# Branch B's k in 512 columns, two merge-gate chunks ahead of branch B's q, and a shorter attention step

## The chip, the core and the metric

The kernel runs on one core of a Trainium2 chip. A core has a matrix engine (TensorE, "PE" in the profile, with a queue of its own for loading weights, "PEld"), a vector engine (VectorE, "DVE"), a scalar engine (ScalarE, "ACT"), GpSimd ("POOL"), and SyncE ("SP"), which here issues every transfer between HBM and the on-chip memory. The engines run at the same time and wait for one another by semaphores. The metric is the device time of one execution in microseconds (us): 963.23 before, the median of three runs (961.96 to 965.53).

## What is computed

One layer of a block with two attention branches, for 1024 positions of width 1024, all in fp32. Cut to what matters:

```python
h = rms_norm(x, norm_w) * (1 + scale) + shift             # scale, shift, gate from c
(cq, ckv, k_rope, gate_a, q_b, k_b, v_b, f_b, gate_b, mg_a, mg_b) = split(h @ w_in)
# branch A: latent attention, 8 heads, chunk-causal
q = rms_norm(cq) @ w_uq ; kv = rms_norm(ckv) @ w_ukv      # then norms per head, rotary parts
y_a = mla_attention(q, kv, k_rope) * silu(gate_a)
# branch B: attention with a forget gate, 8 heads of 64
qb, kb = rms_norm(q_b), rms_norm(k_b)                     # per head
y_b = fox_attention(qb, kb, v_b, log_sigmoid(f_b)) * silu(gate_b)
merged = sigmoid(mg_a) * (y_a @ w_branch_a) + sigmoid(mg_b) * (y_b @ w_branch_b)
x = x + gate * (merged @ w_out)
```

The change touches how `q_b`, `k_b` and `v_b` (512 columns each) and the first of the columns of `gate_a`, `gate_b`, `mg_a`, `mg_b` (24 chunks of 128) are projected, and when.

## The kernel before

**Tiling.** A matrix product is done in three passes: each operand is split into a high and a low part, and high x high, high x low and low x high are summed in one PSUM bank. `split` (L105) makes the parts: ScalarE writes the high part (L115), VectorE subtracts for the low part (L116). The inner dimension of 1024 takes 8 steps, so one output tile costs 24 matmuls. `hT_hi` and `hT_lo` hold the normalized input transposed. Weights are loaded by `load_w` (L102 issues it) into slots of 128x1024 fp32, 0.524 MB.

**Branch B's projection** is the generator `g1b` (L805). q and k are four column chunks of 256 (`ci` 0 and 1 are q, 2 and 3 are k). Each has 8 sequence tiles, two in one bank, so 192 matmuls of 128x256; tile names are `b`. Then come ScalarE's copy (L844) and square (L845) of a 128x512 tile, VectorE's reduction (L849) and, once per chunk, the root (`rsqrt`, L84) and the scaling (L858). The scaled tiles go to DRAM as `qb_d` and `kb_d`. v is one chunk of 512: 8 tiles of 24 matmuls of 128x512, named `bv`, stored as `vb_d`. `store_b` (L891) issues a store only at the next call, and SP issues strictly in the order of the program.

**Order.** It is written out by hand. Attention and the projections of branch A are written as steps. Between them `fill_to(t)` draws matmuls from the generator `fillers` (L924) until a model clock, `pe_time`, which adds up a time for each matmul, reaches `t`. `fillers` yields first all of `g1b`, then 24 chunks `("t", c)` of the gates and merge gates (48 matmuls of 128x512 each, tile `f`), then the chunks of the branch outputs. The order of `g1b` against the steps thus follows from counts of model time.

**Attention** has 16 heads (8 of A, then 8 of B), each of 12 steps. `prep_a` and `prep_b` load a pair of heads' q and k as [positions, columns] (`qs_u`, `ks_u`, 0.524 MB), transpose them on PE (`qt`, `kt`) and, for branch A, load the rotary rows (`q_u` and `k_u` from `qr_d` and `kr_d`, 0.131 MB each). `scores` makes `s`, its maximum, the exponential (ScalarE) and the scaling (GpSimd); `turn` transposes the probabilities (`pt`) and splits them (`pp_u`); the product with v (`v_u`) is `o`. Each step moves the due time on by `STEP` = 2490 model ns, and fill comes up to `due - 600` and `due`. At attention's start, ahead of the fifth score, the rest of `g1b` is drawn whatever the model time (L1281: `while not self.g1b_done: next(self.fill)`). After the last step the rest of the fill runs without a pause.

Of the kernel before, what the change touches and what calls it, by code (L numbers as in the profile page):

```python
# [22 lines left out]
KT = 8  # L23
ST = 8
# [48 lines left out]


class Net:
    STEP = 2490.0

    def __init__(self, ctx, tc, t):
        self.ctx, self.tc, self.nc, self.t = ctx, tc, tc.nc, t
# [725 lines left out]
    def g1b(self, hook):  # L805

        nc, t, U, Hs = self.nc, self.t, self.U, self.Hs
        w = {}

        def load(ci):  # L810
# [5 lines left out]
        load(0)  # L816
        yield False
        w[0] = [self.split(x, f"b0_{e}") for e, x in enumerate(w[0])]
        yield False
        for ci in range(4):  # L820
            kind, half = ci // 2, ci % 2
            for sp in range(4):
                if sp == 0:
                    load(ci + 1)
                if sp in (1, 2) or (ci, sp) == (3, 3):
                    w[ci + 1][sp - 1] = self.split(w[ci + 1][sp - 1], f"b{ci + 1}_{sp - 1}")
                acc = self.fbank(f"b{ci}_{sp}")
                for i in range(2):
                    st = 2 * sp + i
                    sl = slice(st * P, (st + 1) * P)  # L830
                    for kt in range(KT):
                        wh, wl = w[ci][kt // 4]
                        for e, (a, b) in enumerate(((self.hT_hi, wh), (self.hT_hi, wl), (self.hT_lo, wh))):
                            self.mm(acc[:, i * 256:(i + 1) * 256], a[:, kt, sl], b[:, kt % 4],
                                    kt == 0 and e == 0, kt == KT - 1 and e == 2)
                            if (ci, sp, i, kt, e) == (3, 3, 1, 3, 2):
                                U.put(*w[3][0])
                                w[4][3] = self.split(w[4][3], "b4_3")
                            if e == 2 and kt % 2 and (i, kt) != (1, KT - 1):
                                yield False  # L840
                a3 = acc.rearrange("p (g d) -> p g d", d=64)
                o = Hs.get([P, 8, 64], F32, f"bo{ci}_{sp}")
                sq = Hs.get([P, 8, 64], F32, f"bsq{ci}_{sp}")
                nc.scalar.copy(o, a3)  # L844
                nc.scalar.activation(sq, o, AF.Square)  # L845
                if sp == 0:
                    ssq = self.sp.tile([P, 32], F32, tag="bssq", bufs=2, name=f"bssq{ci}")
                    outs = []
                nc.vector.reduce_sum(ssq[:, 8 * sp:8 * sp + 8], sq, axis=AX.X)  # L849
                Hs.put(sq)  # L850
                self.store_b()
                outs.append(o)
                if sp == 3:
                    r = self.rsqrt(ssq, 32, 64, f"b{ci}_{sp}")
                    dst = (self.qb_d, self.kb_d)[kind]
                    items = []
                    for j, o in enumerate(outs):
                        nc.vector.tensor_tensor(out=o, in0=o, op=ALU.mult,  # L858
                                                in1=r[:, 8 * j:8 * j + 8].unsqueeze(2).broadcast_to([P, 8, 64]))
                        items.append((dst[2 * j:2 * j + 2, :, half * 256:half * 256 + 256].rearrange("s p c -> p s c"),  # L860
                                      o.rearrange("p (s h) d -> p s (h d)", s=2), (Hs, o)))
                    self.store_b(*items)
                if sp == 3:
                    for pair in w.pop(ci)[ci // 3:]:
                        U.put(*pair)
                yield 1000.0
        w = w[4]
        for st in range(ST):
            if st in (1, 5):
                hook()  # L870
            acc = self.fbank(f"bv_{st}")
            sl = slice(st * P, (st + 1) * P)
            for kt in range(KT):
                wh, wl = w[kt // 2]
                for e, (a, b) in enumerate(((self.hT_hi, wh), (self.hT_hi, wl), (self.hT_lo, wh))):
                    self.mm(acc, a[:, kt, sl], b[:, kt % 2], kt == 0 and e == 0, kt == KT - 1 and e == 2)
                if st == ST - 1 and kt % 2:
                    U.put(*w[kt // 2])
                if kt < KT - 1:
                    yield False  # L880
            a3 = acc.rearrange("p (g d) -> p g d", d=64)
            vhl = U.get([P, 8, P], F32R, f"bvhl_{st}")
            nc.scalar.copy(vhl[:, :, 0:64], a3)
            nc.vector.tensor_tensor(out=vhl[:, :, 64:128], in0=a3, in1=vhl[:, :, 0:64].bitcast(F32), op=ALU.subtract)
            self.store_b((self.vb_d[st], vhl.bitcast(F32), (U, vhl)))
            if st == ST - 1:
                self.store_b()
                self.g1b_done = True
            yield 1000.0
# [34 lines left out]
    def fillers(self):  # L924

        nc, t, U, Hs = self.nc, self.t, self.U, self.Hs
        chunks = [("t", c) for p in range(8) for c in (p, 8 + 2 * p, 9 + 2 * p)]
        chunks += [(0, d) for d in range(4)] + [(1, d) for d in range(4)]
        w, mg = {}, {}

        def load(k):
            if k < len(chunks):
                kind, c = chunks[k]
                src = t["w_t"][c] if kind == "t" else t["w_br"][kind, c]
                w[k] = self.load_w(src, [P, KT, P], f"f{k}")
# [18 lines left out]

        low, mA = [], {}
        yield from self.g1b(first)
        for pos, (k, u) in enumerate(todo):
            kind, c, e, sh = u
            start = pos == 0 or todo[pos - 1][0] != k
            last = pos + 1 == len(todo) or todo[pos + 1][0] != k  # L960
            if kind == 0 and start and c == 0:
                while not all(isinstance(self.y.get(kk), tuple) for kk in range(4)):
                    yield "wait"
            if start:
                load(k + 1)
# [12 lines left out]
            for i, op in enumerate(ops):  # L978
                if kind != "t":
                    kk, a, b = op  # L980
                    while not isinstance(self.y.get(4 * kind + kk), tuple):
                        yield "wait"
                    op = a[:, 4 * e + kk], self.y[4 * kind + kk][b][:, sl]
# [14 lines left out]
            else:  # L998
                m = mg.pop((kind, c, sh))
# [4 lines left out]
                else:  # L1004
# [249 lines left out]
    def attention(self):  # L1254
# [189 lines left out]
def _chunks(w, kt):  # L1444
    return np.ascontiguousarray(w.reshape(kt, P, w.shape[1]).transpose(1, 0, 2))


def layout(i):
    a = {k: np.asarray(v) for k, v in i.items()}
    f = np.float32  # L1450
    w_in = a["w_in"][0]
    o = {}
# [6 lines left out]
    b = a["b_ada"][0]  # L1459
# [28 lines left out]
    o["w_b"] = np.stack([_chunks(w_in[:, 1184 + 256 * c:1184 + 256 * (c + 1)], 8) for c in range(4)])  # L1488
    o["w_bv"] = _chunks(w_in[:, 2208:2720], 8)
# [28 lines left out]
```

## Time and profile before

| | us |
|---|---|
| median of three runs | 963.23 |
| profiled execution | 961.75 |
| its span in the trace | 959.9 |
| PE busy | 947.9 |
| VectorE busy | 633.2 |
| ScalarE busy | 477.3 |
| GpSimd busy | 208.1 |

The span runs from the first to the last instruction; the profiled execution is 1.85 us longer than it. Busy time of PE is from start to end of matmuls that overlap in the pipeline: how far apart they start, not how long each one takes, is what a stream of them costs. An idle time in brackets names what released the instruction. The attention steps lie between 292 and 810 us. Branch B's projection stands, mixed with branch A's, between the early part and the first scores at 274 us.

### The profile page before, as it was taken

To read this page: it belongs to the slowest core of one execution; us is meant where nothing else is said; L and a number is where in the kernel's file an instruction comes from. 1 tells how busy PE (TensorE), PEld (TensorE's weight loads), DVE (VectorE), ACT (ScalarE), POOL (GpSimd) and SP (SyncE) were. 2 spreads that over 40 slices of the span, in tenths; PEclk is the share of its full clock that TensorE was granted. 3 is DMA by queue.
4 is the path that set the end of the run, shared out by engine and by line. 5 is a ranking of instruction groups with operands and counts; after the bars stand their busy time and mean duration, and the time that the engine had idled before them with its cause. 6 is when DMAs were issued, how large, how long until landed. Compare 5 with 4: busy or idle time off the path is not lost.

```text
span 959.9 us, 14942 instructions
## 1 busy us (share of the span) xinstructions
PE 947.9 (99%) x5390; PEld 820.6 (85%) x5390; DVE 633.2 (66%) x1379; ACT 477.3 (50%) x959; POOL 208.1 (22%) x260
## 2 busy tenths in 40 slices
PE   7999999999999999999999999999999999999998
PEld 7999999998878888888888888888888888888887
DVE  3977877778366667657667676667676766495222
ACT  7776624543245556556555566465565654143000
POOL 0022142200012222221233333232333220046000
PEclk9999999999999999999999999999999999999999
DMA  9831132951973225235332232222421554644321
GB/s 340 334 98 45 51 114 62 323 216 40 343 232 110 88 67 132 71 95 133 99 91 68 66 101 89 80 88 89 120 70 46 186 186 154 238 147 138 103 88 66
DMA packets 79961, 124.96 MB, mean 130 GB/s; under 512 B 5928, under 2 KB 47536, under 8 KB 79888
## 3 DMA queue, kind: packets, MB, share of 16 engines
q1 hardware_dynamic: 79888, 124.01, 39.4%
q8 instruction: 42, 0.69, 0.3%
q14 instruction: 31, 0.25, 0.1%
HBM read 88.33 MB, written 35.66 MB: 129 GB/s over the span
## 4 chain that ended last, share of the span: by engine, by line
PE 92%; DMA 3%; DVE 2%; ACT 2%; issue 1%; SPq 1%; POOL 0%; ACTq 0%; DVEq 0%; POOLq 0%
PE f L127 36%; PE out L127 9%; PE s L127 9%; PE b L127 8%; PE o L127 7%; PE pt L136 6%; PE q L127 3%; PE ckv L127 2%; PE kv L127 2%; PE cq_s L127 2%; PE bv L127 1%; PE cq_t L127 1%; DMA x_u<-in_x 1%; PE pada L127 1%; DMA va_d<-vhl_u 1%
## 5 line engine op out<-in xcount | busy, mean ns | idle before, releaser
L1207 ACT CAST pp_u<-pt 128x512 fp32r<-128x512 f32 x192 | 91.9, 479 | 171.1 <-PE pt L136 155.0
L1208 DVE TENSOR_TENSOR pp_u<-pt,pp_u 128x512 fp32r<-128x512 f32 x192 | 106.7, 556 | 84.8 <-ACT pp_u L1207 81.9
L127 PE MATMUL f<-hT_lo,hi_f_u 128*128 128x512 f32 x384 | 153.6, 400 | 0.0
L127 PE MATMUL f<-hT_hi,lo_f_u 128*128 128x512 f32 x384 | 153.4, 399 | 0.0
L127 PE MATMUL f<-hT_hi,hi_f_u 128*128 128x512 f32 x384 | 153.1, 399 | 0.0
L127 PE MATMUL s<-k_u,q_u 96*128 96x512 f32 (+6 forms) x480 | 116.8, 362 | 0.9 <-DMA k_u<-kr_d 0.9
L1181 DVE TENSOR_REDUCE nm<-s 128x1 f32<-128x128 f32 (+7 forms) x128 | 97.0, 758 | 4.4
L1191 POOL TENSOR_SCALAR p_u<-p_u,rs 128x640 f32<-128x640 f32 (+1 forms) x64 | 64.3, 1004 | 164.1 <-DVE rs L1190 119.0
L1191 POOL TENSOR_SCALAR p_h<-p_h,rs 128x128 f32<-128x128 f32 (+1 forms) x64 | 41.7, 652 | 247.3 <-DVE rs L1190 208.2
L127 PE MATMUL o<-pp_u,v_u 128*128 128x512 f32 (+7 forms) x384 | 94.2, 340 | 0.0
L127 PEld LDWEIGHTS s<-k_u,q_u 96*128 96x128 f32 (+2 forms) x480 | 77.0, 190 | 7.3 <-issue 0.9
L127 PEld LDWEIGHTS f<-hT_hi,hi_f_u 128*128 128x128 f32 x384 | 72.4, 189 | 12.1
L127 PEld LDWEIGHTS f<-hT_hi,lo_f_u 128*128 128x128 f32 x384 | 72.4, 189 | 11.2
L127 PEld LDWEIGHTS f<-hT_lo,hi_f_u 128*128 128x128 f32 x384 | 72.5, 189 | 11.1
L127 PEld LDWEIGHTS o<-pp_u,v_u 128*128 128x128 f32 (+1 forms) x384 | 61.8, 161 | 19.5
L127 PE MATMUL b<-hi_b_u,hT_hi 128*128 128x256 f32 x256 | 73.1, 285 | 0.0
L127 PE MATMUL b<-hi_b_u,hT_lo 128*128 128x256 f32 x256 | 72.4, 283 | 0.0
L127 PE MATMUL b<-lo_b_u,hT_hi 128*128 128x256 f32 x256 | 72.4, 283 | 0.0
L136 PEld LDWEIGHTS pt<-ident,p_u 128*128 128x128 f32 x416 | 52.7, 140 | 16.7
L136 PE MATMUL pt<-ident,p_u 128*128 128x128 f32 x416 | 66.2, 272 | 0.0
L1187 ACT ACTIVATE p_u<-s,nm 128x640 f32<-128x640 f32 (+1 forms) x64 | 61.5, 961 | 4.3 <-DVE nm L1181 3.2
L127 PE MATMUL out<-lo_wo_u,hT_hi 128*128 128x512 f32 (+1 forms) x136 | 51.2, 377 | 0.0
(318 smaller groups left out, 2073.1 us busy)
## 6 DMA issues: line engine op xcount, KB each, us to landing
raw_f_u<-in_w_t SPq DMA_DIRECT2D x24, 512.0 KB
wada_u<-in_w_ada SPq DMA_DIRECT2D x16, 512.0 KB
mg_d<-th_h SPq DMA_DIRECT2D x32, 256.0 KB
mg_h<-mg_d SPq DMA_DIRECT2D x32, 256.0 KB
x_u<-in_x SPq DMA_DIRECT2D x8, 512.0 KB
raw_b_u<-in_w_b SPq DMA_DIRECT2D x8, 512.0 KB
raw_wg_u<-in_w_gate SPq DMA_DIRECT2D x8, 512.0 KB
va_d<-vhl_u SPq DMA_DIRECT2D x8, 512.0 KB
```

The source lines that it names most:

```text
L127: self.nc.tensor.matmul(out, lhsT=l, rhs=r, start=start, stop=stop)
L136: self.nc.tensor.transpose(out=out, in_=in_, identity=self.ident)
L1181: nc.vector.tensor_reduce(out=nm, in_=sv, axis=AX.X, op=ALU.max, negate=True)
L1187: nc.scalar.activation(p[:, 0:w], sv, AF.Exp, bias=nm, accum_out=sm)
L1191: nc.gpsimd.tensor_scalar(out=p[:, 0:w], in0=p[:, 0:w], scalar1=rs, scalar2=0.0, op0=ALU.mult, op1=ALU.add)
L1207: nc.scalar.copy(ph[:, c0:], pt[:, c0:])
L1208: nc.vector.tensor_tensor(out=pl[:, c0:], in0=pt[:, c0:], in1=ph[:, c0:].bitcast(F32), op=ALU.subtract)
```

## The change

Three edits. k of branch B is projected 512 columns wide, tile by tile, from weights `w_bkv` that are laid out like v's (`w_bq` keeps q's two chunks of 256); it is normalized in two groups of four sequence tiles, and stored as whole rows of `kb_d`. Two merge-gate chunks, 23 and 22, come ahead of branch B in `fillers`; branch B follows when they are done. `STEP` is 2376 in place of 2490. The tiles of q are now named `q`, those of k and v both `b`. The core of the diff:

```diff
 class Net:
-    STEP = 2490.0
+    STEP = 2376.0
     def g1b(self, hook):
-            if ci == 4:
-                w[4] = [self.load_w(t["w_bv"][:, 2 * e:2 * e + 2], [P, 2, 512], f"bv_{e}") for e in range(4)]
-            elif ci < 4:
-                w[ci] = [self.load_w(t["w_b"][ci, :, 4 * e:4 * e + 4], [P, 4, 256], f"b{ci}_{e}") for e in range(2)]
+        narrow = lambda c: [self.load_w(t["w_bq"][c, :, 4 * e:4 * e + 4], [P, 4, 256], f"q{c}_{e}") for e in range(2)]
+        wide = lambda m: [self.load_w(t["w_bkv"][m, :, 2 * e:2 * e + 2], [P, 2, 512], f"b{m}_{e}") for e in range(4)]
+
+        def part(w, e):
+            w[e] = self.split(w[e], f"b{e}")
+
+        def normal(dst, outs, ssq, kind):
+            r = self.rsqrt(ssq, 32, 64, f"b{kind}")
...
+            self.store_b(*items)
+
+        def take(acc, name, x, ssq, outs):
...
+            nc.scalar.copy(o, acc.rearrange("p (g d) -> p g d", d=64))
+            nc.scalar.activation(sq, o, AF.Square)
+            nc.vector.reduce_sum(ssq[:, 8 * x:8 * x + 8], sq, axis=AX.X)
+            Hs.put(sq)
+            self.store_b()
-        for ci in range(4):
+        for ci in range(2):
...
+        for m in range(2):
+            for st in range(ST):
+                if m == 0 and st == 5:
+                    nxt = wide(1)
+                if m == 0 and st > 5:
+                    part(nxt, st - 6)
...
+                acc = self.fbank(f"b{m}_{st}")
+                for kt in range(KT):
...
+                        self.mm(acc, a[:, kt, sl], b[:, kt % 2], kt == 0 and e == 0, kt == KT - 1 and e == 2)
+                    if st == ST - 1 and kt % 2:
+                        U.put(*w[kt // 2])
+                        if m == 0 and kt < 4:
+                            part(nxt, 2 + kt // 2)
...
+                else:
+                    take(acc, f"k_{st}", st % 4, ssq, outs)
+                    if st % 4 == 3:
+                        normal(lambda x: self.kb_d[st - 3 + x], outs, ssq, 2)
     def fillers(self):
         chunks = [("t", c) for p in range(8) for c in (p, 8 + 2 * p, 9 + 2 * p)]
+        ahead = 2
+        chunks = [("t", 23 - i) for i in range(ahead)] + [x for x in chunks if x[1] <= 23 - ahead]
...
-        low, mA = [], {}
-        yield from self.g1b(first)
+        low, mA, branch_b = [], {}, self.g1b(first)
+        load(0)
+        yield False
+        w[0] = self.split(w[0], "f0")
+        yield False
         for pos, (k, u) in enumerate(todo):
...
+            if k == ahead and start:
+                yield from branch_b
...
+            if k + 1 == ahead:
+                next(branch_b)
+            elif start:
                 load(k + 1)
```

What it moves is seen in the order of the instructions. First PE, where k ends and v begins. Before (`b` is k, `bv` is v, `hi_b_u` and `lo_b_u` the parts of their weights):

```order
L127 MATMUL b_3_2796<-hi_b_1_u_106_2313,hT_lo 128x256
L127 MATMUL b_3_2796<-hi_b_1_u_106_2313,hT_hi 128x256
L127 MATMUL b_3_2796<-lo_b_1_u_107_2314,hT_hi 128x256
L127 MATMUL b_3_2796<-hi_b_1_u_106_2313,hT_lo 128x256
L127 MATMUL bv_2935<-hi_b_0_u_124_2605,hT_hi 128x512
L127 MATMUL bv_2935<-lo_b_0_u_125_2606,hT_hi 128x512
L127 MATMUL bv_2935<-hi_b_0_u_124_2605,hT_lo 128x512
L127 MATMUL bv_2935<-hi_b_0_u_124_2605,hT_hi 128x512
```

After (`b_7` is the last tile of k, `b_0` the first of v):

```order
L127 MATMUL b_7_2882<-hi_b_u_120_2349,hT_lo 128x512
L127 MATMUL b_7_2882<-hi_b_u_120_2349,hT_hi 128x512
L127 MATMUL b_7_2882<-lo_b_u_121_2350,hT_hi 128x512
L127 MATMUL b_7_2882<-hi_b_u_120_2349,hT_lo 128x512
L127 MATMUL b_0_2942<-hi_b_u_136_2830,hT_hi 128x512
L127 MATMUL b_0_2942<-lo_b_u_137_2831,hT_hi 128x512
L127 MATMUL b_0_2942<-hi_b_u_136_2830,hT_lo 128x512
L127 MATMUL b_0_2942<-hi_b_u_136_2830,hT_hi 128x512
```

k's matmuls are twice as wide, and v's weights are parts of the same form.

Second SP, from the load of the first heads' q (`qs_u`) to that of their k (`ks_u`). Before:

```order
L1054 DMA qs_u_141_3089<-qa_d 128x8x128
L893 DMA vb_d<-bvhl_u_140_3055 128x1024
L893 DMA vb_d<-bvhl_u_142_3094 128x1024
L1156 DMA v_u_144_3149<-va_d 128x8x128
L1062 DMA q_0_u_145_3151<-qr_d 32x1024
L1062 DMA q_0_u_146_3152<-qr_d 32x1024
L1062 DMA q_1_u_147_3155<-qr_d 32x1024
L1062 DMA q_1_u_148_3156<-qr_d 32x1024
L893 DMA vb_d<-bvhl_u_143_3123 128x1024
L1054 DMA ks_u_152_3206<-ka_d 128x8x128
```

After:

```order
L1082 DMA qs_u_138_2874<-qa_d 128x8x128
L912 DMA kb_d<-bok_h_60_2722 128x512
L912 DMA kb_d<-bok_h_64_2825 128x512
L912 DMA kb_d<-bok_h_66_2861 128x512
L912 DMA kb_d<-bok_h_68_2919 128x512
L1184 DMA v_u_146_2974<-va_d 128x8x128
L1090 DMA q_0_u_147_2976<-qr_d 32x1024
L1090 DMA q_0_u_148_2977<-qr_d 32x1024
L1090 DMA q_1_u_149_2980<-qr_d 32x1024
L1090 DMA q_1_u_150_2981<-qr_d 32x1024
L102 DMA raw_f_u_151_2993<-in_w_t 128x1024
L1082 DMA ks_u_152_3023<-ka_d 128x8x128
```

The last four stores of k (`kb_d`) and a weight load (`raw_f_u`) now stand between `qs_u` and `ks_u`; the stores of v (`vb_d`) that stood there come later.

Third PE, at the fourth and fifth scores of the first head (`s_5`, `s_2`). Before (`f` is the first merge-gate chunk):

```order
L127 MATMUL s_5_3349<-k_0_u_156_3225,q_0_u_145_3151 128x384 x2
L127 MATMUL s_5_3349<-k_0_u_157_3226,q_0_u_145_3151 128x384 x2
L127 MATMUL s_5_3349<-k_0_u_156_3225,q_0_u_146_3152 128x384 x2
L127 MATMUL bv_3294<-hi_b_3_u_134_2894,hT_hi 128x512
L127 MATMUL bv_3294<-lo_b_3_u_135_2895,hT_hi 128x512
L127 MATMUL bv_3294<-hi_b_3_u_134_2894,hT_lo 128x512
L127 MATMUL f_00_3373<-hT_hi,hi_f_u_150_3175 128x512
L127 MATMUL f_00_3373<-hT_lo,hi_f_u_150_3175 128x512
L127 MATMUL f_00_3373<-hT_hi,lo_f_u_151_3176 128x512
L127 MATMUL f_00_3373<-hT_hi,hi_f_u_150_3175 128x512
L127 MATMUL s_2_3380<-k_0_u_156_3225,q_0_u_145_3151 128x384
```

After (the run of `b`, which is v, goes on to 96 matmuls before `s_2`):

```order
L127 MATMUL s_5_3170<-k_0_u_156_3043,q_0_u_147_2976 128x384 x2
L127 MATMUL s_5_3170<-k_0_u_157_3044,q_0_u_147_2976 128x384 x2
L127 MATMUL s_5_3170<-k_0_u_156_3043,q_0_u_148_2977 128x384 x2
L127 MATMUL b_4_3184<-hi_b_u_136_2830,hT_hi 128x512
L127 MATMUL b_4_3184<-lo_b_u_137_2831,hT_hi 128x512
L127 MATMUL b_4_3184<-hi_b_u_136_2830,hT_lo 128x512
L127 MATMUL b_4_3184<-hi_b_u_136_2830,hT_hi 128x512
L127 MATMUL b_4_3184<-lo_b_u_137_2831,hT_hi 128x512
```

Before, v ends three matmuls after `s_5` and the chunk `f` begins; now more than half of v is still to come, and it is drawn in one run.

## Rows read from the trace of the kernel before

**Rows 1.** The page, busy time of each engine and its share of the span.
```profile
PE 947.9 (99%) x5390; PEld 820.6 (85%) x5390; DVE 633.2 (66%) x1379; ACT 477.3 (50%) x959; POOL 208.1 (22%) x260
```

**Rows 2.** Busy time of the engines in the stretch of attention (start:end, length, then each engine).
```profile
292.00:810.00 518.00, 517.44 (x2780) 430.92 (x2779) 353.05 (x740) 300.01 (x640) 139.70 (x170) 1.00 0.32 98
```

**Rows 3.** Waits of PE's weight loads, whole span: total us, times, longest us.
```profile
PEld pt L136 <- POOL p_h L1191: 0.5, 1, 0.5
PEld qt L136 <- DVE pp_u L1208: 0.5, 1, 0.5
...
PEld s L127 <- ACT p_h L1187: 0.4, 1, 0.4
...
PEld s L127 <- ACT p_u L1187: 0.2, 1, 0.2
```

**Rows 4.** Timeline of PE, 261 to 276 us: start, duration, engine, line, operation, [idle before].
```profile
261.17 0.60 PE L136 MATMUL qt<-ident,qs_u 128*128 128x128 f32 x4
...
268.25 0.60 PE L136 MATMUL kt<-ident,ks_u 128*128 128x128 f32 x4
...
272.13 0.39 PE L127 MATMUL bv<-lo_b_u,hT_hi 128*128 128x512 f32 x1
...
273.04 0.39 PE L127 MATMUL bv<-hi_b_u,hT_lo 128*128 128x512 f32 x1
273.98 0.30 PE L127 MATMUL s<-k_u,q_u 96*128 96x128 f32 x1 [0.55 <-DMA k_u<-kr_d]
274.62 0.41 PE L127 MATMUL s<-k_u,q_u 96*128 96x128 f32 x2 [0.35 <-DMA k_u<-kr_d]
```

**Rows 5.** Timeline of PE, branch B's k in 256 columns.
```profile
222.02 0.28 PE L127 MATMUL b<-lo_b_u,hT_hi 128*128 128x256 f32 x1
...
222.38 0.28 PE L127 MATMUL b<-lo_b_u,hT_hi 128*128 128x256 f32 x1
```

**Rows 6.** Timeline of PE, branch B's v before its first `lo_b_u` of the last part.
```profile
231.99 0.39 PE L127 MATMUL bv<-hi_b_u,hT_hi 128*128 128x512 f32 x1
233.37 0.50 PE L127 MATMUL bv<-lo_b_u,hT_hi 128*128 128x512 f32 x1 [1.00 <-DVE lo_b_u L116]
```

**Rows 7.** Timeline of ScalarE, a tile of branch B's k.
```profile
229.33 0.58 ACT L844 COPY bo_h<-b 128x512 f32<-128x512 f32 x1
229.94 0.63 ACT L845 ACTIVATE bsq_h<-bo_h 128x512 f32<-128x512 f32 x1
```

**Rows 8.** Timeline of VectorE, the last reduction of branch B's k.
```profile
233.84 0.68 DVE L849 TENSOR_REDUCE bssq<-bsq_h 128x8 f32<-128x512 f32 x1
```

**Rows 9.** Timeline of SP's queue (SPq), 236 to 306 us.
```profile
237.81 2.17 SPq L893 DMA_DIRECT2D kb_d<-bo_h  x4
...
258.38 0.38 SPq L1054 DMA_DIRECT2D ks_u<-ka_d  x1
265.51 0.33 SPq L893 DMA_DIRECT2D vb_d<-bvhl_u  x1
...
267.24 1.88 SPq L1062 DMA_DIRECT2D k_u<-kr_d  x4
...
288.88 1.71 SPq L1062 DMA_DIRECT2D q_u<-qr_d  x4
```

**Rows 10.** Stretches of 237 to 268 us: last columns granted clock, DMA share, GB/s.
```profile
237.00:268.00 31.00, 31.00 (x142) 25.66 (x141) 15.66 (x32) 9.49 (x16) 0.00 (x0) 1.00 0.94 305
239.00:257.00 18.00, 18.00 (x81) 14.92 (x80) 8.37 (x21) 3.85 (x7) 0.00 (x0) 1.00 1.02 365
257.00:268.00 11.00, 11.00 (x54) 9.09 (x53) 5.38 (x8) 4.56 (x8) 0.00 (x0) 1.00 0.94 255
```

**Rows 11.** The same view at the end of the program.
```profile
957.00:959.00 2.00, 0.00 (x0) 0.00 (x0) 0.11 (x1) 0.00 (x0) 0.00 (x0) 0.79 0.20 66
```

**Rows 12.** Timeline of PE, the program's start.
```profile
4.62 5.95 PE L136 MATMUL warm<-ident 128*128 128x128 f32 x32 [4.62 <-DMA ident<-in_ident]
10.41 1.94 PE L136 MATMUL xt<-ident,x_u 128*128 128x128 f32 x16
```

More of the change, by code (lines that the diff above doesn't have):

```diff
@@ new lines, in g1b @@
+        wide = lambda m: [self.load_w(t["w_bkv"][m, :, 2 * e:2 * e + 2], [P, 2, 512], f"b{m}_{e}") for e in range(4)]
[3 more added lines that the diff above has]
+            r = self.rsqrt(ssq, 32, 64, f"b{kind}")
+            items = []
+            for x, o in enumerate(outs):
+                nc.vector.tensor_tensor(out=o, in0=o, op=ALU.mult,
+                                        in1=r[:, 8 * x:8 * x + 8].unsqueeze(2).broadcast_to([P, 8, 64]))
+                items.append((dst(x), o.rearrange("p (s h) d -> p s (h d)", s=2) if kind < 2 else
+                              o.rearrange("p h d -> p (h d)"), (Hs, o)))
+            self.store_b(*items)
@@ L817, in g1b @@
+        def take(acc, name, x, ssq, outs):
+            o, sq = Hs.get([P, 8, 64], F32, f"bo{name}"), Hs.get([P, 8, 64], F32, f"bsq{name}")
+            nc.scalar.copy(o, acc.rearrange("p (g d) -> p g d", d=64))
[3 more added lines that the diff above has]
+            self.store_b()
+            outs.append(o)
+        w = narrow(0)
         yield False
-        w[0] = [self.split(x, f"b0_{e}") for e, x in enumerate(w[0])]
+        for e in range(2):
+            part(w, e)
@@ L819, in g1b @@
         yield False
-        for ci in range(4):
-            kind, half = ci // 2, ci % 2
+        for ci in range(2):
+            outs, ssq = [], self.sp.tile([P, 32], F32, tag="bssq", bufs=2, name=f"bssq{ci}")
             for sp in range(4):
                 if sp == 0:
[L824 to L827, printed above, removed]
+                    nxt = narrow(1) if ci == 0 else None
+                if ci == 1 and sp == 1:
+                    nxt = wide(0)
+                if ci == 0 and sp in (1, 2):
+                    part(nxt, sp - 1)
+                if ci == 1 and sp in (2, 3):
+                    part(nxt, sp - 2)
+                acc = self.fbank(f"q{ci}_{sp}")
@@ L835, in g1b @@
                                     kt == 0 and e == 0, kt == KT - 1 and e == 2)
[L836 to L852, printed above, removed]
-                if sp == 3:
[L854 to L862, printed above, removed]
@@ L863, in g1b @@
-                if sp == 3:
-                    for pair in w.pop(ci)[ci // 3:]:
-                        U.put(*pair)
-                yield 1000.0
[L867 to L889, printed above, removed]
@@ new lines, in g1b @@
+                        if (sp, i, kt) == (3, 1, 3):
+                            U.put(*w[0])
+                            if ci == 1:
+                                part(nxt, 2)
+                        if kt % 2 and (i, kt) != (1, KT - 1):
+                            yield False
+                take(acc, f"{ci}_{sp}", sp, ssq, outs)
+                if sp == 3:
+                    U.put(*w[1])
+                    if ci == 1:
+                        part(nxt, 3)
+                    normal(lambda x: self.qb_d[2 * x:2 * x + 2, :, ci * 256:ci * 256 + 256].rearrange("s p c -> p s c"),
+                           outs, ssq, ci)
@@ L949, in first @@
         def first():
-            if 0 in w:
-                w[0] = self.split(w[0], "f0")
-            else:
-                load(0)
-        low, mA = [], {}
-        yield from self.g1b(first)
+            if ahead in w:
+                w[ahead] = self.split(w[ahead], f"f{ahead}")
+            else:
+                load(ahead)
+        low, mA, branch_b = [], {}, self.g1b(first)
+        load(0)
+        yield False
+        w[0] = self.split(w[0], "f0")
+        yield False
         for pos, (k, u) in enumerate(todo):
@@ L967, in fillers @@
                 load_mg(todo[pos + 1][1])
-            if (last if kind == "t" else (e, sh) == (0, 1)) and k + 1 < len(chunks):
+            if (last if kind == "t" else (e, sh) == (0, 1)) and k + 1 < len(chunks) and k + 1 != ahead:
                 w[k + 1] = self.split(w[k + 1], f"f{k + 1}")
@@ L1487, in layout @@
     o["w_ckv"] = _chunks(w_in[:, 384:640], 8)
-    o["w_b"] = np.stack([_chunks(w_in[:, 1184 + 256 * c:1184 + 256 * (c + 1)], 8) for c in range(4)])
-    o["w_bv"] = _chunks(w_in[:, 2208:2720], 8)
+    o["w_bq"] = np.stack([_chunks(w_in[:, 1184 + 256 * c:1184 + 256 * (c + 1)], 8) for c in range(2)])
+    o["w_bkv"] = np.stack([_chunks(w_in[:, 1696 + 512 * c:1696 + 512 * (c + 1)], 8) for c in range(2)])
     t_cols = [672 + 128 * c for c in range(4)] + [2728 + 128 * c for c in range(4)] + [3240 + 128 * c for c in range(16)]
```

29 lines of the change are left out of this document (22 added, 7 removed).

## The prediction, on record before the result

> **What bounds the kernel now.** I read the busy times of the page first, then the stretches, then the list of waits, then the timelines of the engines between branch B's projections and the first scores. TensorE (PE) is busy for 947.9 of 959.9 us [rows 1], so a term counts only if it shortens PE's own work or makes PE wait. The stretch of attention alone, 518 us, has PE busy for all but 0.6 us, VectorE for 353, ScalarE for 300 and GpSimd for 140 [rows 2]: none of the three bounds it on average. The weight-load queue of PE lists the few waits there, 0.2 to 0.5 us each [rows 3]. The place where PE depends on transfers is the start of attention: the last matmuls of branch B's v, mixed with transposes of q and k, then the first scores; there PE reaches k's transposes without idling, but waits at the first two scores for the rotary rows of k [rows 4]. The edits are priced against the profiled execution, 961.75 us (span 959.9 and 1.85 around it); the median of the runs is 963.23, 1.48 above, and I add the same to my sum.
>
> **k 512 wide.** Removed are 384 matmuls of 128x256, added 192 of 128x512. Three of the narrow ones start 0.36 us apart, so 0.120 each [rows 5]; four of the wide ones 0.91, so 0.2275 [rows 4]. 384 x 0.120 = 46.1 against 192 x 0.2275 = 43.7: -2.4 us. A step of 0.01 us in the reading of 0.36 moves this by 1.3, so -1.1 to -3.7. Copies, squares and reductions stay equal in number and size (128x512 each), so they cost nothing new.
> The Trainium skill, "TensorE: Matmul & The Clock Gate", section "Back-to-back issue gap", gives an isolated matmul N/2.4 + 2.5 ns of spacing. By that, as an estimate, the narrow one would take 109 ns, the wide one 216, and the edit would save 0.4 us; the rows show 120 and 228 here, so the measured pitches decide.
>
> **v's weights.** Before, the fourth part of v's weights is split late: PE starts a matmul at 231.99 and the next, which needs the low half, at 233.37 [rows 6], 1.38 less the pitch 0.23 = 1.15 us lost. In the new order v's parts are split during k's last tile, the last of them with 12 of its wide matmuls still ahead and 18 of v's first tile behind, before its use: 30 x 0.2275 = 6.8 us of cover, against about 5.5 before (18 wide, 12 narrow). 1.3 more covers 1.15: -1.15, and 0 if DVE's queue grows by as much.
>
> **k's stores and the load that k's transposes need.** This is the large term. SP issues in program order, and the new order puts the last four `kb_d` stores between `qs_u` and everything that attention's start loads. Let K be the end of k's last matmul. Then ScalarE copies (0.58) and squares (0.63) [rows 7], with the hand-over some 1.5 us in all, and DVE reduces, takes the root and scales. Before, the last such reduction starts at 233.84 [rows 8] and the first store goes out at 237.81 [rows 9]: 3.97. So the first new store goes out at K+5.5, and, as four take 2.17 [rows 9], SP is free at K+7.6. Behind it stand `v_u` (about 0.4, as `ks_u` takes 0.38), four `q_u` (1.71), one `raw_f_u` (0.4), and then `ks_u`, issued at K+10.2 [rows 9]. PE runs 24 matmuls of v after K, 5.47 us, and then the same instructions that took from 261.17 to 268.25 before, 7.08 [rows 4]: it wants `ks_u` at K+12.55.
> When does it land? From K+5.5 the queue holds four stores of 0.262 MB, `v_u` 0.524, four `q_u` of 0.131, `raw_f_u` 0.524 and `ks_u` 0.524: 3.15 MB. This stretch moved 305 GB/s at a DMA share of 0.94 [rows 10]: 10.3 us. What lies around the bytes I take from before's own case: the store issued at 265.51, two gate loads and the first `k_u` (1.70 MB, 5.6 us at 305) were usable at 273.98, 8.47 later, so 2.9 [rows 4, 9]. Landing is at K+5.5+10.3+2.9 = K+18.7, a wait of 6.1 us at `kt`. Bounds: 365 GB/s, the best part of the stretch, gives 4.4; 255, the worst, 8.2 [rows 10]; with nothing ahead of it, `ks_u` alone takes 2.9 + 1.7 from K+10.2, a wait of 2.2. I take +6.1, the rate of the whole stretch. Before, `ks_u` had 268.25 - 258.38 = 9.9 us and just served; now it has 2.4.
> The Trainium skill, "DMA: Bandwidth & Descriptors", section "Anatomy of one DMA", has 2.0 us plus the bytes over 436 GB/s; as an estimate this would land the 3.15 MB at K+14.7, a wait of 2.1. Here no stretch in the rows passes 365 over several microseconds, so I leave the page's figure to the rival below.
>
> **The clock behind that wait.** At the end of the program, from 957 to 959 us, PE does nothing, and the granted clock is 0.79 of full on average [rows 11]: if it falls to the lower of its two levels (1.2 of 2.4 GHz), it does so at (1 - 0.79) x 2 x 2 us = 0.84 before the end of that stretch. A 6 us wait at `kt` gives it far more idleness than the 1.2 us before that. What coming back costs: the first 32 transposes of the program, after 4.62 us of idleness, took 5.95 us, the next 16 took 1.94 [rows 12]; at the later pace ((1.94 - 0.28) / 15 = 0.111) 32 would take 3.7. So +2.3, bounds 0 (the clock stays) and 3 (all of PE's work up to the first scores, 5 us, at half the pace, less the next term).
>
> **The rotary rows of k.** Before, the scores wait 0.7 and 0.35 us for them [rows 4]. They come 1.70 MB behind `ks_u`, 5.6 us at 305 GB/s, while PE takes 5.0 from `kt` to the first score, 7.3 with the slower clock. With it the wait goes: -1.0. Without, it stays about as it is: 0.
>
> **The two chunks ahead.** 96 matmuls move from later to the start; at 0.2275 they are 21.9 us of work there and here. The 96 matmuls of v forced out before the fifth score are PE work too. Both cost nothing as long as PE has the operands. Early, though, q's first weights must be split just before q starts: no matmul of branch B's q waited before, so there is nothing to win and the lower bound is 0; the upper is 1.4, one wait the size of that in rows 6. I take +0.5, nearer to none.
>
> **The shorter steps.** 192 steps take 518 us, 2.70 each, for a model step of 2.490; the new one, 2.376, makes 2.57, so 0.123 less each. A chain from scores to transposes that spans two steps loses 0.25. Four waits on such chains stand in the list: `pt` for `p_h` 0.5, `qt` for `pp_u` 0.5, `s` for `p_h` 0.4 and `p_u` 0.2 [rows 3]. Each grows by 0.25, 1.0 in all, and I allow 0.8 for chains that just fit now: +1.8; 0 if they are single events, 4 if each of 16 heads has one.
>
> **Sum.** -2.4 - 1.15 + 6.1 + 2.3 - 1.0 + 0.5 + 1.8 = +6.15: 967.9 for the profiled execution, 969.4 on the median.
>
> **Rivals.** (1) The queue keeps up. The stores drain at once and only `ks_u` itself counts: a wait of 2.2 and no fall of the clock: -2.4 - 1.15 + 2.2 + 0.5 + 1.8 = +1.0, 964.2. For it: 365 GB/s at times, and `ks_u` was never seen late. Against: DMA share 0.94 over 31 us [rows 10]; transfers were queueing, and `k_u` was late.
> (2) The steps bind. Softmax falls behind in every head, not in four places: another 16 x 0.25 = +4: 973.4. For it: the four waits exist at the longer step. Against: the other engines have a third of the stretch free [rows 2].
> (3) Faster. SP's wait for the scaled k is harmless, because the scaling is done by about K+2 (it decides if the first store goes out before then, so that `ks_u` lands by K+12.55): -2.4 and -1.15 remain, and nothing else: -3.55, 959.7; with the wait of the scores gone too, 958.6. For it: DVE has slack on average. Against: 3.97 us from the reduction to the first store is a chain of small operations that nothing in the edit shortens.
>
> **How the numbers follow.** My forecast 0.55, rival 1 0.20, rival 2 0.12, rival 3 0.13. Half a per cent, 4.8 us, is about what a measurement of this kernel can tell from no change. The forecast's own range is 966.5 to 972 (wait 4.4 to 8.2, the other terms near their values), four fifths of it over 968.05: 0.43, and with rival 2 slower is 0.55. Faster, under 958.4, needs rival 3 with a little more: 0.05. The same: 0.40. The range 962 to 974 holds the forecast, rival 1 and most of rival 2, and leaves rival 3 and the far tail out.
>
> **What would show it.** In the new profile: `kt` with an idle time of 4 to 8 us, released by `ks_u`; SP waiting for the scaled k before `v_u`; a granted clock under 1 just behind; 192 k matmuls 0.2275 apart; no wait of v for `lo_b_u`; waits of `pt` and `s` in attention a little longer than the four in the list. If `kt` does not wait, or under 2 us, my main step is wrong and the time is near 960 to 964; if attention's stretch is not shorter by some 20 us, the steps are set by something else than PE.

## The result: 973.15 us, and the profile after

The changed kernel takes 973.15 us (median of 6 runs, 970.81 to 974.64), the kernel before 964.18 in runs beside it: a ratio of 1.0084 (95% interval 1.0064 to 1.0105). It is slower by some 8 to 9 us (8.1 by the ratio, 9.0 by the medians); 969.4 was forecast, in a range of 962 to 974. The profiled execution is 973.75 us with a span of 972.0. That is 12 us above the one of before, since that one lay at the low end of its runs and this one in the upper half; the parts below add up to these 12.

The page (its span and the busy times) answers to [rows 1]:

```profile
span 972.0 us, 14548 instructions
...
PE 948.5 (98%) x5198; PEld 810.7 (83%) x5198; DVE 637.3 (66%) x1379; ACT 477.2 (49%) x959; POOL 204.1 (21%) x260
```

PE is as busy as before, 948 us, but its share of the span falls: it is idle for 23.5 us, where it was for 12.0, so nearly all of the loss is waiting. The list of PE's waits (engine, line, waited for: total us, times, longest), where before nothing but the program's start was over 1.0 us:

```profile
PE kt L136 <- DMA ks_u<-ka_d: 6.7, 1, 6.7
...
PE kv L127 <- ACT hi_ukv_u L118: 2.1, 1, 2.1
...
PE s L127 <- ACT p_h L1215: 1.1, 2, 0.7
PE q L127 <- DVE lo_b_u L116: 0.9, 1, 0.9
PE pt L136 <- DVE pp_u L1236: 0.9, 1, 0.9
```

Three of these were in the forecast's sum (`kt`, `q` and those of attention: `s`, `pt`). The second, `kv` for `w_ukv`, was not.

**The main term.** PE's timeline where `kt` stands, for [rows 4]:

```profile
270.05 0.39 PE L127 MATMUL b<-hi_b_u,hT_lo 128*128 128x512 f32 x1
277.17 1.09 PE L136 MATMUL kt<-ident,ks_u 128*128 128x128 f32 x4 [6.74 <-DMA ks_u<-ka_d]
...
278.49 0.63 PE L127 MATMUL b<-lo_b_u,hT_hi 128*128 128x512 f32 x1
278.91 0.63 PE L127 MATMUL b<-hi_b_u,hT_lo 128*128 128x512 f32 x1
...
281.48 0.60 PE L136 MATMUL kt<-ident,ks_u 128*128 128x128 f32 x4
...
284.01 0.45 PE L127 MATMUL s<-k_u,q_u 96*128 96x128 f32 x3
```

The matmul before starts at 270.05, `kt` at 277.17: 7.12 less a pitch of 0.23, so 6.9 us lost, against 6.1 forecast. After it the wide matmuls start 0.42 apart (278.49, 278.91) and not 0.23, and the two groups of `kt` are 4.31 us apart. Before, they were 2.52 apart (the first at 268.25 [rows 4]), so the clock costs 1.8 us, against 2.3:

```profile
270.77 0.60 PE L136 MATMUL kt<-ident,ks_u 128*128 128x128 f32 x4
```

The granted clock of the changed kernel (third figure from the end; then DMA share and GB/s) shows the same:

```profile
276.00:278.00 2.00, 0.83 (x5) 0.86 (x5) 0.00 (x0) 0.00 (x0) 0.00 (x0) 0.50 1.03 416
...
280.00:282.00 2.00, 2.00 (x10) 1.61 (x10) 1.22 (x2) 0.00 (x0) 0.00 (x0) 0.76 1.04 213
282.00:284.00 2.00, 2.00 (x10) 1.61 (x9) 0.46 (x1) 1.37 (x2) 0.00 (x0) 1.00 1.01 326
```

It stands at half, the lower level of the two, when PE starts again, and is full from 282 us on; that it would fall, the forecast took from the end of the program [rows 11]. The first score, 284.01, waits no more for `k_u`, as forecast. SP's queue shows why `ks_u` is late, for [rows 9]:

```profile
252.94 0.77 SPq L1082 DMA_DIRECT2D qs_u<-qa_d  x1
263.21 2.13 SPq L912 DMA_DIRECT2D kb_d<-bok_h  x4
...
268.51 0.43 SPq L1082 DMA_DIRECT2D ks_u<-ka_d  x1
...
272.04 2.94 SPq L1090 DMA_DIRECT2D k_u<-kr_d  x4
```

`qs_u` goes out at 252.94, and the next issue is 10 us later: SP waits for the scaled k (`bok_h`), with `v_u`, `q_u` and `ks_u` behind it (in e1, below, these go out from 257.5 on). SP's list of waits between 245 and 275 us, same columns as PE's, has it first:

```profile
SPq L912 <- DVE bok_h L818: 9.6, 4, 9.0
```

The first store goes out 5.5 us after v's first matmul (257.75), just as worked out from K. `ks_u` follows at 268.51, 5.3 us after the first store, where 4.7 was worked out, and PE can use it 14.0 us after that store, where 13.2 was.

**k 512 wide.** Ten pitches of the wide k, for [rows 5]:

```profile
239.62 0.39 PE L127 MATMUL b<-lo_b_u,hT_hi 128*128 128x512 f32 x1
...
241.89 0.39 PE L127 MATMUL b<-hi_b_u,hT_lo 128*128 128x512 f32 x1
```

2.27 / 10 = 0.227 us each. 192 of them are 43.6 us, where 384 at 0.120 were 46.1: -2.5, against -2.4. v's wait for its last weights [rows 6] is gone, 1.16 us.

**Attention.** From the first `pt` to the last `o` there were 516.8 us before and are 495.9 now: 20.8 less, where 192 steps that are 0.123 shorter make 23.6. The difference is about what the new waits there come to (2.9, in the table below). Its busy times, for [rows 2]:

```profile
322.50:818.50 496.00, 493.90 (x2672) 410.49 (x2671) 350.02 (x732) 294.41 (x630) 135.02 (x170) 1.00 0.33 97
```

PE is idle for 2.1 of the 496 us, where it was for 0.6 of 518.

### The profile page after: what moved, and what is told of

Same layout as the page of the kernel before. It is cut to its first block, busy times and chain, and to the rows that moved or that the text cites. A ratio compares the mean times of both kernels' runs of the same rounds, so it can differ in the third digit from the quotient of the medians.

```text
span 972.0 us, 14548 instructions
## 1 busy us (share of the span) xinstructions
PE 948.5 (98%) x5198; PEld 810.7 (83%) x5198; DVE 637.3 (66%) x1379; ACT 477.2 (49%) x959; POOL 204.1 (21%) x260
## 4 chain that ended last, share of the span: by engine, by line
PE 89%; DMA 4%; DVE 3%; ACT 2%; issue 1%; POOL 1%; SPq 1%; DVEq 0%; POOLq 0%; ACTq 0%
PE f L127 33%; PE out L127 9%; PE b L127 9%; PE s L127 8%; PE o L127 7%; PE q L127 6%; PE pt L136 6%; PE ckv L127 2%; PE kv L127 2%; PE cq_s L127 2%; PE cq_t L127 1%; DMA ks_u<-ka_d 1%; DMA raw_ukv_u<-in_w_ukv 1%; PE kt L136 1%; DMA x_u<-in_x 1%
## 5 line engine op out<-in xcount | busy, mean ns | idle before, releaser
L1219 POOL TENSOR_SCALAR p_h<-p_h,rs 128x128 f32<-128x128 f32 (+1 forms) x64 | 36.8, 575 | 256.4 <-DVE rs L1218 236.6
L1215 ACT ACTIVATE p_u<-s,nm 128x640 f32<-128x640 f32 (+1 forms) x64 | 61.5, 961 | 11.7 <-DVE nm L1209 9.7
L116 DVE TENSOR_TENSOR lo_f_u<-raw_f_u,hi_f_u 128x512 fp32r<-128x512 f32 x64 | 47.7, 785 | 10.6 <-ACT hi_f_u L115 10.5
L127 PE MATMUL out<-hi_wo_u,hT_lo 128*128 128x512 f32 (+1 forms) x136 | 51.3, 377 | 0.0
L127 PE MATMUL out<-hi_wo_u,hT_hi 128*128 128x512 f32 (+1 forms) x136 | 51.2, 377 | 0.0
```

The lines of the kernel that those rows point to most:

```text
L116: engine.tensor_tensor(out=lo[:, ks], in0=raw[:, ks], in1=hi[:, ks].bitcast(F32), op=ALU.subtract)
L127: self.nc.tensor.matmul(out, lhsT=l, rhs=r, start=start, stop=stop)
L1215: nc.scalar.activation(p[:, 0:w], sv, AF.Exp, bias=nm, accum_out=sm)
L1219: nc.gpsimd.tensor_scalar(out=p[:, 0:w], in0=p[:, 0:w], scalar1=rs, scalar2=0.0, op0=ALU.mult, op1=ALU.add)
```

## What was not foreseen: the load of w_ukv

Branch A's `kv` matmuls wait for the scaled parts of `w_ukv`:

```profile
187.28 0.40 PE L127 MATMUL kv<-hi_ukv_u,ckvTl_u 128*128 128x512 f32 x1
189.76 0.50 PE L127 MATMUL kv<-hi_ukv_u,ckvTh_u 128*128 128x512 f32 x1 [2.08 <-ACT hi_ukv_u L118]
190.54 0.50 PE L127 MATMUL kv<-lo_ukv_u,ckvTh_u 128*128 128x512 f32 x1 [0.29 <-DVE lo_ukv_u L119]
```

SP's queue ahead of them, in the changed kernel:

```profile
168.82 2.14 SPq L102 DMA_DIRECT2D raw_b_u<-in_w_bkv  x4
...
172.67 1.53 SPq L766 DMA_DIRECT2D qa_d<-qraw_u  x2
180.39 1.51 SPq L102 DMA_DIRECT2D raw_ukv_u<-in_w_ukv  x2
```

In the kernel before:

```profile
170.79 1.20 SPq L766 DMA_DIRECT2D qa_d<-qraw_u  x2
173.66 1.40 SPq L102 DMA_DIRECT2D raw_ukv_u<-in_w_ukv  x2
```

And ScalarE in the changed kernel, which scales the second half (L118):

```profile
188.98 1.33 ACT L118 ACTIVATE hi_ukv_u<-raw_ukv_u,vec 128x512 fp32r<-128x512 f32 x2 [2.97 <-DMA raw_ukv_u<-in_w_ukv]
```

The four loads of k's weights (`raw_b_u<-in_w_bkv`, 2.1 MB) now go out ahead of the stores `qa_d` and of `raw_ukv_u`. SP then waits for a store of `qa_d` to land, since the load takes over its slot. SP's list of waits:

```profile
SPq L102 <- DMA qa_d<-qraw_u: 6.0, 1, 6.0
```

So `raw_ukv_u` goes out 7.7 us after `qa_d` (172.67 to 180.39); before it was 2.9 (170.79 to 173.66). The scaling of the second half starts at 188.98, and PE loses 3.05 us at `kv` (2.25, 0.56 and 0.24 above the pitch). The size is that of one execution: in the profile of e8 (below), whose program is the same up to attention, `kv` loses 1.0 us.

## The experiments

The time that PE loses at a place is counted "over the pitch": the distance of two starts less the usual distance of such a pair of matmuls in these runs, where it exceeds 0.15 us; attention is counted from the fourth score to the last `o`. All times are medians; the kernel before had 964.69, 962.87 and 962.74 beside them in the three groups (e1 to e4, e5 to e8, e9 to e11), and 964.18 beside the changed kernel. Runs of different groups are therefore compared by their ratios to the kernel before; 0.001 of a ratio is about 1 us.

**e1: `ks_u` ahead of the stores.** The four stores of k are held back until v's second tile, so that `ks_u` is issued first.

```diff
-                    self.store_b((self.vb_d[st], vhl.bitcast(F32), (U, vhl)))
+                    if st == 0:
+                        self.pending_b = (*self.pending_b, (self.vb_d[st], vhl.bitcast(F32), (U, vhl)))
+                    else:
+                        self.store_b((self.vb_d[st], vhl.bitcast(F32), (U, vhl)))
```

> The changed kernel, with the last four kb_d stores held back until ks_u has been issued; nothing else moves. Theory A (SP's order makes the wait at kt: ks_u is issued only after the scaled k): the idle time of kt, 6.7 us in the changed kernel, goes to under 1, and with it the 1.8 us of matmuls at half clock behind it; the stores then stand ahead of k_u, so up to 1 us may come back at the first score. 973.2 - 8.7 + 0.5 = 965.0. Rival B (the queue is full at that time whatever the order): kt still waits 3 us or more for ks_u, the clock still falls, 969 or more.

969.86 us, where A expected 965.0: 3.3 less than the changed kernel by the medians, 2.2 by the ratios (1.0061 for 1.0084). PE there:

```profile
272.34 0.60 PE L136 MATMUL kt<-ident,ks_u 128*128 128x128 f32 x4
...
277.78 0.44 PE L127 MATMUL s<-k_u,q_u 96*128 96x128 f32 x1 [2.77 <-DMA k_u<-kr_d]
```

`kt` does not wait any more: its lateness came from SP's order, as A has it. But 2.8 us of the wait have moved to the first score, and behind it the clock is at half again (0.50 from 278 to 282 us). SP's queue:

```profile
260.56 0.43 SPq L1085 DMA_DIRECT2D ks_u<-ka_d  x1
262.69 2.30 SPq L915 DMA_DIRECT2D kb_d<-bok_h  x4
...
269.07 2.50 SPq L1093 DMA_DIRECT2D k_u<-kr_d  x4
```

`ks_u` goes out at 260.56, 8 us earlier; `k_u` now stands behind the stores and goes out at 269.07. So A named the right place, and not all of the cause.

**e2: w_ukv ahead of half of k's weights.**

```diff
-        wide = lambda m: [... for e in range(4)]
+        wide = lambda m, es=range(4): [... for e in es]
...
                 if ci == 1 and sp == 1:
-                    nxt = wide(0)
+                    nxt = wide(0, (0, 1))
+                if ci == 1 and sp == 2:
+                    nxt += wide(0, (2, 3))
```

> The changed kernel, with two of the four loads of k's weights (w_bkv) issued behind the load of w_ukv. Theory C (the changed kernel's new wait of branch A's kv matmuls for w_ukv, 3.0 us over the pitch, is made by the 2.1 MB of k's weights that stand ahead of it): with half of them ahead it falls to under 1, 973.2 - 2.5 = 970.7, and kt waits as before, since all behind moves together. Rival D (it is the slot or the scaling on ScalarE that is late): the wait stays within 0.5 us, 973.

970.04 us: 3.1 less than the changed kernel by the medians, 2.2 by the ratios (1.0061). SP's queue, and the one wait on a transfer that is left behind the program's start:

```profile
168.96 1.16 SPq L102 DMA_DIRECT2D raw_b_u<-in_w_bkv  x2
...
173.62 4.35 SPq L102 DMA_DIRECT2D raw_ukv_u<-in_w_ukv  x2
...
```

```profile
PE kt L136 <- DMA ks_u<-ka_d: 6.3, 1, 6.3
```

`raw_ukv_u` goes out 2.4 us after `qa_d` (171.23) and `kv` waits no more, so the order of these loads made all of its wait, as C has it. The edit moves two things at once, though: the bytes ahead of `w_ukv`, and the slot that its load takes over, since slots are handed out in turn (SP now waits 3.1 us there for a store of `qr_d`, where it waited 6.0 for `qa_d`). No run tells the two apart. `kt` keeps its wait.

**e3: both.**

> Both edits together. If theories A and C hold and add: 973.2 - 8.2 - 2.5 = 962.5, at or a little below the kernel before (964.2). If B or D: between 968 and 973.

968.09 us, ratio 1.0041, where 962.5 was expected if A and C held and added up. By the ratios the two edits gain 2.2 us each and 4.1 together, by the medians 3.3, 3.1 and 5.1; differences across the groups are uncertain by some 2 us, so the times do not tell whether the two gains add. The trace shows why the 962.5 is missed. First the wait at the scores, then the stretches from 240 us (the last figures: granted clock, DMA share, GB/s):

```profile
PE s L127 <- DMA k_u<-kr_d: 5.1, 2, 4.9
```

```profile
240.00:275.00 35.00, 32.45 (x150) 26.27 (x149) 25.10 (x54) 16.52 (x28) 0.00 (x0) 1.00 1.05 324
...
278.00:282.00 4.00, 3.79 (x11) 2.99 (x11) 1.57 (x5) 1.04 (x3) 0.00 (x0) 0.50 0.35 135
```

PE comes to the scores 2.2 us earlier than in e1 (272.6 and 274.9 us) and waits 5.1 us there, while `kt` waits 0.4. The DMA share was 1.05 on average over 240 to 275 us: the queue was full. So neither A alone nor B holds: SP's order decides which transfer is late, and with the order mended what is late is `k_u`, behind the stores in a full queue. Whether the bytes ahead of it are the reason is what e5 asks.

**e5: the stores behind `k_u`.** As e3, with the stores held for two tiles of v.

```diff
-                    if st == 0:
+                    if st < 2:
                         self.pending_b = (*self.pending_b, ...
```

> The two edits of e3, and the held stores (four kb_d, one vb_d, 1.57 MB) go out only after k_u's loads. In e3 kt waits 0.5 us over the pitch, the first two scores 5.3, and the clock at half behind them costs another 1.7: 7.5 us. Theory G (the queue is full from 240 us on, and what counts is the bytes ahead of ks_u and k_u): 1.57 MB at 305 GB/s are 5.1 us fewer ahead of k_u, so the scores wait under 1 us, the clock stays at full, and the time is 968.1 - 6.7 = 961.4. Rival H (k_u's own small rows are slow, whatever stands ahead): the scores still wait 3 us or more, 965 or more.

962.34 us (ratio to before 0.9990, 0.9978 to 1.0003). SP's queue:

```profile
258.42 0.43 SPq L1087 DMA_DIRECT2D ks_u<-ka_d  x1
...
261.84 2.82 SPq L1095 DMA_DIRECT2D k_u<-kr_d  x4
...
267.94 4.59 SPq L917 DMA_DIRECT2D kb_d<-bok_h  x4
```

`k_u` goes out at 261.84, in e3 it was 267.45; neither `kt` nor the first scores wait any more, and the clock stays at full. (Early on, `ltckv` and q still lose the 1.0 and 1.1 us that they lose in the changed kernel.) By the ratios (1.0041, 0.9990) e5 is 4.9 us under e3, where G expected 6.7. H falls: with 1.57 MB fewer ahead of them, the small rows of `k_u` are there in time. Against the kernel before, e5 shows no difference.

**e6: q's weights earlier, raw_f behind `ks_u`.**

```diff
-                if m == 1 and st in (1, 5):
+                if m == 1 and st in (2, 5):
...
-            if k + 1 == ahead:
+            if (k, sh) in ((0, 1), (1, 0)):
                 next(branch_b)
-            elif start:
+            if k + 1 != ahead and start:
```

> As e5, and q's first weights are loaded and split half a chunk earlier, and the merge-gate chunk's load raw_f is issued behind ks_u. The wait of q's first matmul for lo_b_u, 1.1 us over the pitch in every run since the change, goes; raw_f moves 0.52 MB from ahead of ks_u to ahead of k_u. By G 961.4 - 1.1 - 0.3 = 960.0; by H 964.

962.31 us, where 960.0 was expected. q's wait of 1.1 us is gone, but in the profiled execution (964.77, the longest of its twelve; the shortest was 960.52) the scores lose 2.8 us over the pitch, and the clock falls. PE's first score, and the stretch behind it:

```profile
273.45 0.30 PE L127 MATMUL s<-k_u,q_u 96*128 96x128 f32 x1 [2.09 <-DMA k_u<-kr_d]
```

```profile
274.00:276.00 2.00, 1.93 (x6) 1.67 (x7) 1.10 (x4) 0.00 (x0) 0.00 (x0) 0.50 1.04 396
```

PE reaches the scores 1.3 us sooner than in e5, with as many bytes ahead of `k_u`. That alone does not make 2.8 us: `k_u` itself came at least 1 us later than in e5 (after 273, where it was there by 272.5), though it was issued 0.3 us sooner. Why is not shown. e5 had little to spare at the scores: in e9 (below), with the same order, they wait 0.2 us for `k_u`.

**e4: the step alone.** The kernel before with `STEP = 2376.0`.

> The kernel before, with only STEP = 2376 in place of 2490. Theory E (the shorter step itself makes the new waits in attention, 4.2 us over the pitch in the changed kernel against 1.3 before): the same 3 us appear here, 964.2 + 2.9 = 967. Rival F (they come from the moved work or the disturbed start of attention): no more than 1 us, 964 to 965; the fill that attention no longer takes is run behind it without a gap and costs nothing.

979.14 us, 14.5 above before; 2.9 was expected by E, 1 at most by F, so both miss. Over the pitch attention loses 7.4 us, 1.3 before. And behind it, PE at the end of the steps:

```profile
793.81 0.39 PE L127 MATMUL f<-hi_y_u,lo_f_u 128*128 128x512 f32 x1
801.83 0.80 PE L127 MATMUL f<-hi_y_u,hi_f_u 128*128 128x512 f32 x1 [7.63 <-DVE mA_u L1003]
```

Attention ends with more of the fill still to come, 363 matmuls of `f` in place of 261. All of them make the branch outputs (`hi_y_u` is a part of their inputs). There PE waits 7.6 us for VectorE's accumulation into `mA_u`, which is held up behind the load and split of the last `y`; the clock falls again. The cost of a step is thus not a matter of the step alone: it sets where every later piece of the fill meets attention. In the changed kernel 271 matmuls of `f` are left at the end, and this stall does not occur. Their number alone does not decide it: e8 (below) has 339 left and loses 0.8 us there, e7 has 249 and loses 3.8 with the clock.

**e7 and e8: a longer and a shorter step.** e7 is e6 with `STEP = 2400.0`, e8 the changed kernel with `STEP = 2300.0`.

> As e6 with STEP 2400 in place of 2376. Theory E (attention's waits grow with the step's shortness): the waits over the pitch in attention fall from about 4 to about 3, and the time by 1: 959. Rival I (they sit at single places that the step does not set): 960, as e6.

> The changed kernel with STEP 2300: steps of 2.49 us in place of 2.57. Theory E: the waits in attention, 4.2 us over the pitch at 2376, rise to 7 or more, 976 or more if the end of the fill keeps up, and some us more if it waits for y as in e4. Rival I: attention waits the same 4 us, 973.

e7 takes 971.32 us, e8 977.40. Over the pitch attention loses 9.4 us at 2400 and 7.4 at 2300, against 4.2 at 2376 (3.9 in e6). e8 went as E said; e7 went the other way from E, and not as I either. The longest waits of e7, 292 to 830 us:

```profile
PE qt L136 <- DVE pp_u L1241: 2.3, 2, 1.2
PE s L127 <- ACT p_h L1220: 2.2, 4, 0.7
PE f L127 <- DVE mA_u L1036: 2.1, 1, 2.1
PE f L127 <- DVE lo_y_u L116: 1.3, 1, 1.3
```

The waits rise on both sides of 2376: one per cent more costs 9 us (e6 to e7; 3.8 of them at the end, where PE waits for `mA_u` as in e4 and the clock falls), three per cent less 4 by the medians and 7 by the ratios (the changed kernel to e8). No run has the changed order with the old step of 2490, so how much of attention's new waits is the step's and how much the order's stays open.

**e9, e10: the split in mid-chunk.** To e5 and e7:

```diff
-            if (last if kind == "t" else (e, sh) == (0, 1)) and k + 1 < len(chunks) and k + 1 != ahead:
+            due = (last if kind == "t" else (e, sh) == (0, 1)) and k + 1 < len(chunks) and k + 1 != ahead
+            if due and kind != "t":
                 w[k + 1] = self.split(w[k + 1], f"f{k + 1}")
...
                 self.mm(acc, *op, i == 0, i == len(ops) - 1)
+                if due and kind == "t" and i == 8:
+                    w[k + 1] = self.split(w[k + 1], f"f{k + 1}")
```

> As e5, with one edit in the fill: the split of the next chunk's weights (1.14 us of ScalarE, 1.29 of VectorE) comes after the ninth matmul of a chunk's last half and not ahead of the first, where the previous half's tanh and gate stand too. Theory J (attention's waits come from a chunk's end: its tanh, gate and split fall into one step, and where a step also prepares q or k, the probabilities are late; the step's length only sets where they meet): the waits over the pitch in attention, 3.6 us in e5, fall under 1.5, and 962.3 goes to 960.2. Rival E (the step is too short for its own softmax): the waits stay within 1 us of 3.6, 962.

> As e7 (STEP 2400), with the same edit of the split. E said that the longer step waits less, and e7 showed more, 9 us over the pitch. Theory J: with the split apart these fall under 5, and the time from 971.3 to 967 or less. Rival K (the longer step runs the fill further, and it is the fill's own operands and the end of the fill that are late): attention's waits stay over 8, 970 or more.

e9 takes 961.41 us, 0.9 under e5 where 2.1 was expected (ratios 0.9982 and 0.9990, which their intervals do not tell apart); e10 takes 971.85, no better than e7. In e9 attention still loses 3.5 us over the pitch, at other places than in e5 (3.6); in e10 it loses 9.1 (9.4 in e7). J falls in both: to move the split moves the waits, and does not remove them. The numbers are those of the rivals, E for e9 and K for e10; but E has e7 against it, and of K's late operands the list of e10 has only 1.3 us (`lo_y_u`) in attention and 2.4 (`mA_u`) at its end. So which coincidence sets the waits stays open.

**e11: what helped, together,** and the two gate loads ahead of `k_u` put behind it:

```diff
-            if i == 2:
+            if i == 3:
                 self.gate_load((4, 5))
```

> STEP 2376 with all that helped: w_ukv ahead of half of k's weights, k's stores after k_u, q's weights earlier, raw_f behind ks_u, the split in mid-chunk, and the two gate loads that stand ahead of k_u put behind it (1.05 MB less ahead of the scores). G and J: no wait at kt or at the scores, none of q, attention under 1.5: 962.3 - 1.1 - 2.1 = 959.1, 0.4% under the kernel before. If J falls 961.

959.85 us, ratio to before 0.9964 (0.9949 to 0.9979): faster than the kernel before and than the changed one; 959.1 was expected, or 961 if J fell. Its page:

```profile
span 958.9 us, 14579 instructions
...
PE 946.2 (99%) x5198; PEld 810.4 (85%) x5198; DVE 634.8 (66%) x1379; ACT 478.3 (50%) x959; POOL 210.1 (22%) x260
```

No wait on a transfer is left after the program's start, and the clock is full up to the end of the first scores; the longest wait in attention is 0.7 us. Against the changed kernel PE's last matmul ends 13.1 us earlier (954.9 for 968.0). What each edit gives of this was not measured one by one; the move of the gate loads in particular was not run alone.

## Why the prediction came out as it did

The direction and the main mechanism were right. The sum was not: of 11.7 us it had 6.15. The median, 973.15, lies 0.85 us inside the upper end of the stated range, and outside the forecast's own range (966.5 to 972); the room above that had been left for steps that bind in every head, which is not what happened. That the time came inside is in part luck. By steps, in the profiled executions:

| step | forecast | measured |
|---|---|---|
| k 512 wide | -2.4 | -2.5 |
| v's wait for its weights | -1.15 | -1.16 |
| `kt` waits for `ks_u` | +6.1 | +6.9 |
| clock behind it | +2.3 | +1.8 |
| scores no longer wait for `k_u` | -1.0 | -1.0 |
| early stage: q's weights | +0.5 | +1.1 (and 0.6 more at `ltckv`) |
| shorter steps | +1.8 | +2.9 |
| `kv` waits for `w_ukv` | none | +3.05 |
| sum | +6.15 | +11.7 |

PE's last matmul ends 11.8 us later (956.2, 968.0), so the table is nearly whole. Each figure is read from one execution.

- **k's stores.** Right in place, cause and nearly in size: SP stood still for 10 us until branch B's k was scaled, and the loads for branch A's first head stood behind these stores. e1 showed that the order alone is not the whole: with it mended the same stretch of the queue was too full for `k_u`. The rate that the sum used, 305 GB/s, was close to the 324 that e3 had under a full queue; the rival by which the queue keeps up (a wait of 2.2 and no fall of the clock) is out. So is the estimate that stood beside it, worked out from the Trainium skill ("DMA: Bandwidth & Descriptors", section "Anatomy of one DMA"): a wait of 2.1 us, where the trace has 6.9. The Trainium skill gives that figure for one DMA issued from GpSimd; here SP issued eleven, one behind the other.
- **The clock.** Right: half when PE came back, for about 4 us. One reading behind it was short: in the kernel before, PE's last matmul ended at 956.2 and the clock fell at about 958.2 (worked out from [rows 11]), so PE had been idle for 2.0 us by then, not for 1.2. Other runs showed the half clock behind shorter waits as well (below).
- **What failed** is the step on the moved work, "Both cost nothing as long as PE has the operands", with only q's weights named as late. The later branch B, with a wide k that asks for four loads at once where there were two, has these loads ahead of `w_ukv`, in a stage that the forecast did not look at; SP's order shows it as plainly as it shows the stores. With q's weights and `ltckv` this term measured 4.75 us in place of 0.5, and `w_ukv` alone is a quarter of the loss.
- **The steps.** The size was near (2.9 for 1.8), the reason was not borne out. The forecast held that a shorter step takes 0.25 us from each chain; e7 and e8 showed waits that rise on both sides of 2376. The rival by which the steps bind in every head is out: the list has six waits there, not sixteen.
- **The faster rival** needed the first store within 2 us of K; it went out at K+5.5. With the waits on transfers mended, e11 is 3.5 us under before by its ratio, and 3.55 had been worked out for this rival. That the two agree is partly chance: e11 also gains the wait of the first scores, about 1 us, and loses some 2 us more than before in attention, and the 3.55 counts neither.

## What to carry to other kernels

When work is moved, follow the queue that issues the transfers through every stage that the move passes, not only through the one where the work lands: here a store that waited for its data held up all loads behind it, and a block of early loads delayed the small one that was needed first. Mending the order was half of it: look then at whether the queue is full, and put what is needed late (stores, gate weights) behind what is needed next. A due time that is fitted to one order of the fill has to be looked at again once the order changes.

## What had not been expected

- The half clock came after 2.8 us of idle PE in e1, where it cost 1.9 us, two thirds of the wait itself, and after 2.1 us in e6 and in e7; behind the 6.7 us of `kt` it cost 1.8. But it does not always come: after the 2.1 us at `kv` in the changed kernel and after 2.4 us at the end of e10 the granted clock stayed at 1.00.
- SP's wait for a slot, 6.0 us for `qa_d`, was a wait for a store that stood behind 2.1 MB of loads: the reuse of a buffer tied this load to the queue ahead of that store.
- One per cent in the step's due time, 2376 to 2400, cost 9 us (e6 to e7), as much as the whole change did.
